# Masked softmax: the batches whose stores go out as a half and two quarters end with batch 5 instead of batch 7

## The chip, the cores and the metric

One core of a Trainium2 chip. The metric is the device time of one execution in microseconds (us), the median of several runs. The granted clock is 1.0 in all runs, and all are in the fast state, but for two of the four runs with stores of 64 partitions, which are said where they come.

A packet is one record of a DMA engine in the trace. A transfer has landed when the last of its semaphore records is in.

## The reference, cut to what matters

```python
batch, heads, seq_q, seq_k = 16, 8, 256, 256
x       = randn(batch, heads, seq_q, seq_k)            # float32
lengths = randint(seq_k // 2, seq_k, size=batch)
for b in range(batch):
    m = x[b, :, :, :lengths[b]]
    m = exp(m - max(m, axis=-1))
    result[b, :, :, :lengths[b]] = m / sum(m, axis=-1)  # zero beyond the length
```

One batch is 2 MB: 128 partitions of 16 rows of 256 values. It is loaded, masked, exponentiated, divided by its row sums and stored.

## The kernel before: the parts that matter

All loads and stores pass through eight slots in on-chip memory. Loads 0 to 3 are issued by the sync engine in full width. Loads 4 to 15 are issued by GpSimd, in a width rounded up from the batch's length, so their rows are short. Stores are issued by the sync engine, which waits for the division and, at the start of a batch, for the store of two batches before.

```python
def parts(b):
    if b == 0:                 cuts = [0, nt]
    elif b < 8:                cuts = [0, half, half + quarter, nt]   # nt = 16 rows
    elif b != batch - 3:       cuts = [0, half, nt]
    else:                      cuts = [0, nt]
    return [slice(i, j) for i, j in zip(cuts, cuts[1:])]
# ... (cut)
for b in range(batch):                                   # sync engine
    s_b = s_st[b % 2]
    for s in parts(b):
        nc.sync.wait_ge(s_out, 2 * b + (s.stop - 1) // half + 1)      # L117: divided
        if b >= 2 and s.start == 0:
            nc.sync.wait_ge(s_b, 64 * (b // 2 + 1))                   # L119: store b-2 landed
        nc.sync.dma_start(out=out_f[b, :, s, :], in_=xt[:, b % slots, s, :]   # L120
            ).then_inc(s_b, 16 * ((s.stop - s.start) // quarter))
# ... (cut) VectorE: the mask (L195) waits for the load; the division (L222) for the exponentials
for b in range(batch):
    at = 0 if b == batch - 2 else 2 if b == batch - 3 else 1 if b == 0 or b >= ahead else 0
    for h in range(3):
        if h == at and b + 1 < batch:
            mask(b + 1, slice(0, nt))
        if h < 2:
            divide(b, h)
```

The two quarters of a batch wait for the same count of `s_out`: neither can go before the other's rows are divided, and they differ from one half only in how the transfer is cut. Note `at`: batch 15 is masked before batch 14 is divided.

The softmax here doesn't subtract the row's maximum and nothing guards it: scores larger than these inputs give would overflow.

## Time and profile before

| | before |
|---|---|
| time, median of 3 runs | 156.04 us (155.91 to 156.53) |
| profiled span | 154.3 us |
| busy share of the 16 DMA engines, stores' queue and loads' queue | 66.0% and 32.2% |
| VectorE, ScalarE busy | 75%, 68% |

These two lines of the page before give GB/s in each of the 40 slices of the span, and the packets:

```profile
GB/s 117 427 450 420 437 365 409 400 408 452 407 406 390 415 404 417 412 413 415 405 419 413 414 412 405 416 416 420 417 416 423 418 431 435 418 444 418 423 431 130
DMA packets 10132, 62.08 MB, mean 402 GB/s; under 512 B 866, under 2 KB 962, under 8 KB 6290
```

No slice between the first and the last falls under 365. "Under 8 KB" holds the 4096 B packets of the quarters and the packets of the short-row loads. The prediction tells these apart by their records in the trace.

### The profile page before, as it was taken

Reading aid. Unit: us, or ns where it says so; the run is one execution under the profiler, and the core shown is the slowest. Engines: PE = TensorE matmul, PEld = TensorE weight load, DVE = VectorE, ACT = ScalarE, POOL = GpSimd, SP = SyncE. Lnnn points to the kernel's source line nnn. Section 1 sums busy time; section 2 is a strip of 40 time slices with the busy share of each in tenths; the row PEclk is TensorE's granted clock in tenths of the full one; section 3 lists DMA queues with packets and bytes.
Section 4 is the critical chain, followed back from the end, with each engine's and each line's share of the span. In section 5 each row is a group of like instructions: output and inputs, shape, how many; then the busy total and the mean of one; then the engine's idle time right before and its main releaser. Section 6 shows DMA issues by size and latency. Waiting matters only on the chain.

```text
span 154.3 us, 1325 instructions
## 1 busy us (share of the span) xinstructions
PE 0.2 (0%) x1; PEld 0.1 (0%) x1; DVE 115.4 (75%) x84; ACT 105.2 (68%) x514; POOL 19.0 (12%) x25
## 2 busy tenths in 40 slices
PE   0000000000000000000000000000000000000000
PEld 0000000000000000000000000000000000000000
DVE  1339999952999696988969696969698692599500
ACT  3097799992592969779595959596877907988000
POOL 4910031000320200202011020202010000000000
DMA  4999999999999999999999999999999999999993
GB/s 117 427 450 420 437 365 409 400 408 452 407 406 390 415 404 417 412 413 415 405 419 413 414 412 405 416 416 420 417 416 423 418 431 435 418 444 418 423 431 130
DMA packets 10132, 62.08 MB, mean 402 GB/s; under 512 B 866, under 2 KB 962, under 8 KB 6290
## 3 DMA queue, kind: packets, MB, share of 16 engines
q1 hardware_dynamic: 6048, 41.95, 66.0%
q0 software_dynamic: 4080, 20.12, 32.2%
q14 instruction: 2, 0.02, 0.0%
q10 hardware_dynamic: 2, 0.00, 0.0%
HBM read 28.51 MB, written 33.55 MB: 402 GB/s over the span
## 4 chain that ended last, share of the span: by engine, by line
DMA 54%; DVE 25%; issue 7%; ACT 5%; ACTq 2%; SPq 1%; POOLq 1%; DVEq 0%
DMA xt<-in_x_dram 33%; DMA out_dram<-xt 21%; DVE xt L222 14%; DVE xt L195 9%; ACT xt L251 5%; ACTq L251 1%; DVE inv_sum L219 1%; SPq L109 1%; POOLq L99 0%; SPq L120 0%; SPq L111 0%; DVEq L212 0%; POOLq L130 0%; POOLq L135 0%; ACTq L246 0%
## 5 line engine op out<-in xcount | busy, mean ns | idle before, releaser
L251 ACT ACTIVATE xt<-xt x256 | 102.3, 401 | 35.2 <-DVE xt L195 35.2
L222 DVE TENSOR_TENSOR xt<-xt,inv_sum 128x2048 f32<-128x2048 f32 x32 | 73.4, 2292 | 1.1
L195 DVE SCALAR_TENSOR_TENSOR xt<-down,len_s,xt 128x2048 f32<-128x2048 f32 (+1 forms) x17 | 37.8, 2221 | 14.1 <-DMA xt<-in_x_dram 14.0
L251 ACT ACTIVATION_READ_ACCUMULATOR xt<-xt x256 | 47.9, 187 | 0.0
L130 POOL DMA_DIRECT2D xt<-in_x_dram x12 | 12.8, 1064 | 94.6 <-issue 48.7
L219 DVE RECIPROCAL inv_sum<-row_sum 128x8 f32<-128x8 f32 x32 | 6.3, 198 | 12.1 <-ACT xt L251 12.1
L149 POOL MEMSET xt<- 128x1536 f32 x4 | 5.3, 1386 | 1.1 <-DVE len_s L186 1.1
L243 ACT ACT_TABLE_LOAD x1 | 1.3, 1283 | 1.6 <-SPq L81 1.6
L178 DVE TENSOR_SCALAR down<-iota_i 128x256 f32<-128x256 int32 x1 | 0.3, 297 | 1.6 <-POOL iota_i L141 1.6
L183 DVE CAST len_b<-word 1x16 bf16<-1x16 int32 x1 | 0.2, 164 | 0.4 <-DMA word<-in_lengths_dram 0.4
L186 DVE TENSOR_SCALAR len_s<-len_f 128x16 f32<-128x16 f32 x1 | 0.2, 174 | 0.4 <-PE len_f L165 0.4
L141 POOL IOTA iota_i<- 128x256 int32 x1 | 0.3, 332 | 0.6 <-SPq L81 0.6
L146 POOL MEMSET seed<- 1x1 f32 x2 | 0.3, 162 | 0.0
L243 ACT ACTIVATE warm<-const-float32-0.0 128x1 f32<-128x1 f32 x1 | 0.2, 203 | 0.0
L144 POOL MEMSET ones<- 1x128 bf16 x1 | 0.2, 194 | 0.0
L165 PE MATMUL len_f<-len_b,ones 1*128 1x16 bf16 x1 | 0.2, 168 | 2.6 <-DVE len_b L183 2.6
L274 POOL MEMSET const-float32-0.0<- 128x1 f32 x1 | 0.1, 98 | 0.3 <-issue 0.3
L165 PEld LDWEIGHTS len_f<-len_b,ones 1*128 1x128 bf16 x1 | 0.1, 97 | 2.6 <-POOL ones L144 2.6
L274 POOL MEMSET const-float32-1.0<- 128x1 f32 x1 | 0.1, 98 | 0.0
L274 POOL MEMSET const-bfloat16-1.0<- 128x1 bf16 x1 | 0.1, 98 | 0.0
L274 POOL MEMSET const-uint8-127<- 128x1 uint8 x1 | 0.1, 98 | 0.0
L274 POOL BASE_LOAD x1 | 0.0, 17 | 0.1
## 6 DMA issues: line engine op xcount, KB each, us to landing
out_dram<-xt SPq DMA_DIRECT2D x21, 1024.0 KB
out_dram<-xt SPq DMA_DIRECT2D x14, 512.0 KB
xt<-in_x_dram SPq DMA_DIRECT2D x3, 2048.0 KB, 16.0
xt<-in_x_dram POOLq DMA_DIRECT2D x3, 1728.0 KB, 16.5
out_dram<-xt SPq DMA_DIRECT2D x2, 2048.0 KB
xt<-in_x_dram POOLq DMA_DIRECT2D x2, 2048.0 KB, 18.4
xt<-in_x_dram POOLq DMA_DIRECT2D x2, 1600.0 KB, 16.7
xt<-in_x_dram POOLq DMA_DIRECT2D x2, 1280.0 KB, 14.5
```

The source lines that it names most:

```text
L109: nc.sync.dma_start(out=xt[:, 0, s], in_=x_f[0, :, s]).then_inc(s_ld[h], 16)
L130: nc.gpsimd.dma_start(out=xt[:, slot, :, :w], in_=x_n[:, n, :, :w]).then_inc(s_sw[par], 16)
L141: nc.gpsimd.iota(iota_i, pattern=[[1, seq_k]], base=0, channel_multiplier=0).then_inc(s_iota, 1)
L146: nc.gpsimd.memset(seed[:, par : par + 1], 0.0).then_inc(s_st[par], 64)
L149: nc.gpsimd.memset(xt[:, b, :, low:], 0.0).then_inc(s_fill, 1)
L165: nc.tensor.matmul(len_f, lhsT=ones, rhs=len_b, start=True, stop=True).then_inc(s_lenf, 1)
L195: return nc.vector.scalar_tensor_tensor(out=t, in0=down[:, None, lo:hi].to_broadcast([P, s.stop - s.start, hi - lo]), scalar=len_s[:, b : ...
L219: step(nc.vector.reciprocal(out=inv_sum[:, b, s], in_=row_sum[:, b, s]))
L222: nc.vector.tensor_tensor(out=t, in0=t, in1=inv_sum[:, b, s, None].to_broadcast([P, half, seq_k]), op=ALU.mult,).then_inc(s_out, 1)
L243: nc.scalar.activation(out=warm, in_=nc.const_aps.tensor(0.0, (P, 1), F32), func=EXP)
L251: ins = nc.scalar.activation(out=e, in_=e, func=EXP, accum_out=sum_h[:, bass.ds(i, 1), j])
L274: nc = _bacc.Bacc("TRN2", target_bir_lowering=False, num_devices=1)
```

## The change

Intent: two transfers fewer, and larger packets, in batches 6 and 7. The whole diff:

```diff
-        elif b < 8:
+        elif b < 6:
             cuts = [0, half, half + quarter, nt]
```

## The prediction

> **What bounds the kernel now.** I read the page first, then the waits, the busy time by stretch, and the chain of waits at the end.
>
> From the page:
>
> ```profile
> span 154.3 us, 1325 instructions
> DMA  4999999999999999999999999999999999999993
> q1 hardware_dynamic: 6048, 41.95, 66.0%
> q0 software_dynamic: 4080, 20.12, 32.2%
> out_dram<-xt SPq DMA_DIRECT2D x21, 1024.0 KB
> out_dram<-xt SPq DMA_DIRECT2D x14, 512.0 KB
> ```
>
> The 16 DMA engines are full in 38 of 40 slices, and the two queues fill 98.2% of the span. So 62 MB of traffic is the bound, and only what leaves the DMA engines empty, or makes packets dearer, can cost time. q1 carries the first four loads and then all stores; q0 carries the other twelve loads. The 14 stores of 512 KB are the quarters of batches 1 to 7.
>
> The waits, of the engines and of the queue that issues stores:
>
> ```profile
> DVE xt L195 <- DMA xt<-in_x_dram: 14.0, 4, 4.8
> SPq L119 <- DMA out_dram<-xt: 91.7, 14, 9.6
> SPq L120 <- DVE xt L222: 12.6, 9, 3.3
> ```
>
> VectorE waits for a load only four times. The store issuer waits mostly for the store of two batches before (L119): stores stand in a backlog, and compute runs ahead of them.
>
> The chain of waits, its last stretch:
>
> ```profile
> 115.19 17.53 DMA xt<-in_x_dram
> 132.95 2.35 DVE xt L195
> ...
> 135.45 2.29 DVE xt L222
> ...
> 137.89 2.29 DVE xt L222
> ...
> 140.33 2.29 DVE xt L222
> ...
> 142.77 2.29 DVE xt L222
> ```
>
> Here that changes. The last load (batch 15) lands at 132.72 us, and the mask and four divisions of batches 14 and 15 follow without a gap up to 145.06, which is 12.34 us after the landing. The last store is issued at 145.09. By the trace's semaphore records it lands at 153.08, 8.0 us later, because batches 13 and 14 are still ahead of it in the queue. The first load, a 1 MB half on an empty queue, needed 1.13 to 6.20, or 5.07 us. So the last store has about 8.0 - 5.07 = 2.9 us of **slack**: the last load can be that much later before the end moves. This rests on the estimate that a lone 1 MB store takes as long as that lone 1 MB load.
>
> **How the queues share the engines.** The trace's packet records show a store packet of 8192 B for a half (mean 313 ns) and of 4096 B for a quarter (163 ns), and load packets of about 4.4 KB (171 to 177 ns) made of several short rows. In 50 to 100 us I count 2038 store packets and 2160 load packets; in 100 to 120 us, with halves alone, 647 and 690. The ratio is 1.06 and 1.07[...]. So the size of a store packet decides who gets the bandwidth. While a quarter is being stored, loads get about half; while a half is, about a third.
>
> [...]
>
> ```profile
> 84.00:89.37 5.37, 0.00 (x0) 0.00 (x0) 4.19 (x4) 5.37 (x29) 0.00 (x0) 1.00 1.03 415
> 93.46:98.90 5.44, 0.00 (x0) 0.00 (x0) 4.26 (x4) 4.77 (x24) 1.15 (x1) 1.00 1.03 410
> 98.90:102.85 3.95, 0.00 (x0) 0.00 (x0) 3.37 (x3) 2.74 (x14) 0.00 (x0) 1.00 1.01 413
> 102.85:106.84 3.99, 0.00 (x0) 0.00 (x0) 3.36 (x3) 3.75 (x20) 1.15 (x1) 1.00 1.02 419
> ```
>
> The first two stretches run from the landing of a batch's half to that of its second quarter (batches 6 and 7), the last two are the halves of batch 8. The last column is GB/s: 410 to 415 against 413 to 419, nearly the same total, but the same 1 MB of stores takes 5.4 us in quarters and 3.97 us as a half. [...]
>
> **The change, part by part.**
>
> Removed: for batches 6 and 7, four quarter stores become two halves, so two issues fewer on the sync engine (about 0.4 us each when not held up, by the trace). That engine waits 91.7 us for stores; this is worth nothing. Both quarters wait for the same division (the wait rounds up to the whole second half), so no store starts earlier or later because of the form itself.
>
> Packets: 512 packets of 4096 B become 256 of 8192 B, 16 fewer pairs per engine: 16 x (2 x 163 - 313) = 16 x 13 ns = **0.2 us** less DMA work over the whole kernel. This is the whole direct gain.
>
> Moved: stores of the second halves of batches 6 and 7 go at 3.97 instead of 5.4 us, so batch 7 lands about 2.9 us sooner (96.0 instead of 98.9). Loads pay. In 83.3 to 88.5 and 92.8 to 98 us, quarters against loads, each engine took 15.94 + 15.75 load packets in 10.4 us: 328 ns each. From 98.9 to 122.8, halves against loads, all engines took 829 in 23.87 us: 461 ns each. The quarters run beside about 32 x 1.07 = 34 load packets per engine. With halves these need 34 x (461 - 328) = **4.5 us** more. I take 4.6, since a count of pure turns (32 x (3.97/8 - 5.4/16) us) gives 5.1.
>
> Does the loss stay? Loads get it back only if the store queue runs empty. After the change batch 8 is issued at about 88 (batch 6 landed, division done at 85.55), batch 9 at 96 and so on; each store issue still finds about one batch queued. Only the masks are held up: loads 10 and 11 land some 2.3 and 3.5 us later, loads 12 to 15 4.6 us later. Load 10 landed 0.8 us before its mask, load 13 0.5 us and loads 14 and 15 right at it, so VectorE now waits for every load from 10 on. The divisions of batches 9 to 12 ended 3.8 us or more before their stores were issued; now the stores are due 2.9 us sooner and the masks come 2 to 4.5 us later, so batches 11 and 12 can be issued 1 to 4 us late. But one whole batch (8 us) is in flight at each issue, so the queue doesn't run dry there. By conservation, loads and the stores up to batch 12 are both done by about 138.1, as they are before (batch 12 lands at 138.28); what has changed is that the loads come last with them instead of 5 us earlier.
>
> At the end: last load at 132.72 + 4.6 = 137.3; last division at 137.3 + 12.34 = 149.7; last store lands at 149.7 + 5.07 = 154.8 instead of 153.08. That is 4.6 - 2.9 = **+1.7 us**. By then only batch 13 is queued: it ends at about 138.1 + 4.95 = 143.1 (it took 138.28 to 143.24), and the halves of 14 and 15 come at the pace of the divisions (2.44 us each), which is just that of the DMA. So the engines run out of work once, when batch 13 has drained and the first half of 14 is only being issued, around 143 to 145.
>
> Sum: 156.04 + 1.7 = 157.7 us. The 0.2 us of saved packets falls before the last load and could take a little off; a slow engine or a store slower than a load could add. I say **157.7 us**.
>
> **Rivals.** *Hidden anyway:* the end is set by total traffic; with 0.2 us less work it would be 155.8. For it speak 38 full slices and 2.9 us of slack; against it, that the loss of 4.6 us is larger than the slack. It needs the loads to lose less than 2.9 us. *Whole loss on the path:* if the slack is mostly an artefact [...] or the store queue runs dry in the 110s because masks come late, the end moves by 3.5 to 4.6 us: 159.5 to 160.6. Against it: the batch in flight at each issue. *Fewer, larger stores are faster:* [...] 1% of the rate over the 10.8 us of quarters would be 0.1 us. Even the mixed stage at 413 and the later one at 418 GB/s differ in load widths too. It cannot reach 2%.
>
> **Range and chances.** The loss of loads is 4.0 to 5.1 us, the slack 2 to 3.2 us, so the end moves by 0.8 to 3.1, and for what I have not seen (loads catching up in a gap of the store queue) I go lower: 156.4 to 159.1. The 2% mark is 159.16, which needs the second rival in part: 0.09. Faster by 2% needs 152.9 us, below the traffic bound: 0.01. Within 2%: 0.90.
>
> **What would show it.** Right: 35 stores instead of 37, 23 of 1024 KB and 10 of 512 KB; the same load landings up to about 83 us; the wait of the mask (L195) for loads up from 14.0, with more than four times; the last load landing near 137.3; the last store landing some 5 us after its issue, with a DMA slice below 9 near 143. The load share of the traffic from 83 to 98 us falls from about half to a third. Wrong: if load 15 lands before about 135.6, the end should not move; if it lands at 137 and the end still doesn't move, a lone store is faster than 5 us; if the time rises by 4 us, the slack was none.

The sum is 156.04 + 1.7 = 157.7 us, with 1.7 = 4.6 - 2.9 from the trace's counts and times and from the estimate that a lone store takes as long as a lone load. The "pure turns" of the 5.1 us are an estimate too: exactly one load packet to one store packet, where 1.06 and 1.07 were counted. By the packet records, loads moved 51% of the bytes beside quarters (83.3 to 88.5 us) and 37% beside halves (98.9 to 122.8 us). The lines that follow a cut there without a word before them are busy time by stretch, with GB/s last.

## The result and the profile after

Ratios are the mean time of one kernel's fast runs over that of the other's of the same rounds, so not quite the ratio of the medians.

| | before | after |
|---|---|---|
| time, median | 156.18 us (155.91 to 156.53, 4 runs) | 158.0 us (157.91 to 158.38, 4 runs) |
| ratio | | 1.012 (95%: 1.009 to 1.015) |
| profiled span | 154.3 us | 156.8 us |
| last load lands | 132.72 us | 139.10 us |
| last store lands (its issue) | 153.08 (145.09) | 155.52 (151.47) |
| store of batch 7 lands | 98.90 | 95.91 |
| store of batch 12 lands | 138.28 | 138.57 |

Landings are from the semaphore records of the trace. The change costs 1.8 us of the median: 1.2%, inside 2%. The profiled run is the slowest of the four (158.38).

From the page after:

```profile
span 156.8 us, 1323 instructions
DMA  3999999999999999999999999999999999991995
GB/s 111 424 443 422 443 406 414 395 404 443 405 399 401 391 413 423 406 419 407 413 429 407 420 417 412 413 413 420 420 412 425 414 416 449 424 443 63 426 410 226
DMA packets 9844, 62.08 MB, mean 396 GB/s; under 512 B 834, under 2 KB 930, under 8 KB 5746
out_dram<-xt SPq DMA_DIRECT2D x23, 1024.0 KB
out_dram<-xt SPq DMA_DIRECT2D x10, 512.0 KB
```

The bytes are the same. The transfers are fewer by two, as they should be. The full row of nines now has a hole: slice 37 (from 141.1 to 145.0 us) at "1" and 63 GB/s.

Busy time by stretch, after (last two columns: DMA share and GB/s). The first two stretches are the second halves of batches 6 and 7, now one transfer each; the last two are the hole and what follows it:

```profile
84.07:88.06 3.99, 0.00 (x0) 0.00 (x0) 2.80 (x3) 3.99 (x21) 0.00 (x0) 1.00 1.02 420
91.83:95.91 4.08, 0.00 (x0) 0.00 (x0) 4.04 (x3) 1.51 (x7) 1.16 (x1) 1.00 1.02 415
143.02:144.99 1.97, 0.00 (x0) 0.00 (x0) 1.94 (x3) 1.97 (x11) 0.00 (x0) 1.00 0.00 0
145.00:155.20 10.20, 0.00 (x0) 0.00 (x0) 6.38 (x5) 3.43 (x18) 0.00 (x0) 1.00 0.98 408
```

The halves take 4.0 and 4.1 us, where the quarters took 5.4, at nearly the same total rate (415 to 420 GB/s, and 410 to 415 before). For 1.97 us nothing moves at all; then 4 MB of stores go out.

The waits after, of VectorE and of the sync engine:

```profile
DVE xt L195 <- DMA xt<-in_x_dram: 19.5, 8, 5.3
```

```profile
SPq L119 <- DMA out_dram<-xt: 75.6, 13, 8.6
SPq L120 <- DVE xt L222: 34.9, 17, 5.5
```

Before, the mask waited four times for a load (14.0 us in all); now eight times. The store issuer still waits most for earlier stores (75.6 us, 91.7 before), but 34.9 us for divisions instead of 12.6: stores now wait in part for loads.

The chain of waits after, its last stretch:

```profile
121.09 18.01 DMA xt<-in_x_dram
...
139.33 2.35 DVE xt L195
...
149.15 2.29 DVE xt L222
```

It is the same chain as before, 6.4 us later: load 15, the mask, four divisions. It takes 12.34 us from the landing to the last division, to the hundredth what it took before (151.44 - 139.10).

Where did the time go? By the packet records from 83 to 98 us, loads moved 2.95 MB before and 2.32 MB after, stores 3.22 and 3.96 MB. The sum is the same within 2%; the loads' part falls from 48% to 37%. At the end, the loads that were pushed back finish together with the store of batch 12, and only one 2 MB store is left to cover the chain that follows the last load. It isn't long enough: the store queue is empty from 143.02 us, and the first half of batch 14 is issued at 144.15.

### The profile page after: what moved, and what is told of

It reads as the page before. It is cut to its first block, busy times and chain, and to the rows that moved or that the text cites. A ratio compares the mean times of both kernels' runs of the same rounds, so it can differ in the third digit from the quotient of the medians.

```text
span 156.8 us, 1323 instructions
## 1 busy us (share of the span) xinstructions
PE 0.2 (0%) x1; PEld 0.1 (0%) x1; DVE 115.9 (74%) x84; ACT 105.2 (67%) x514; POOL 19.0 (12%) x25
## 4 chain that ended last, share of the span: by engine, by line
DMA 79%; DVE 8%; issue 5%; POOLq 3%; SPq 1%; POOL 0%; DVEq 0%
DMA xt<-in_x_dram 79%; DVE xt L222 6%; DVE xt L195 2%; POOLq L99 1%; POOLq L135 1%; POOLq L130 1%; SPq L109 1%; POOL xt L130 0%; DVE inv_sum L219 0%; SPq L111 0%; POOLq L157 0%; POOLq L153 0%; POOLq L159 0%; POOLq L137 0%; DVEq L212 0%
```

## The experiments

**Theory A**: about one load packet moves per store packet, of 4096 B as of 8192 B (1.06 from 50 to 100 us, where 1315 of 2038 store packets have 4096 B, and 1.07 from 100 to 120 us, where all have 8192 B), so the size of a store packet sets the loads' share; the end moves only by what the loads lose beyond a slack at the end. Rivals: B, a cost in proportion to the batches in halves; C, the number or size of transfers matters, not their packets; others below. All results were correct. Ratios are against the kernel before on the same chip.

### Half of the change

```diff
-        elif b < 8:
+        elif b < 7:
```

> Half of the change: quarters end with batch 6, so only batch 7 goes in halves. Theory A (a store packet's size sets the loads' share; the end moves only by the loads' loss beyond the slack at the end): the loads lose half of what they lost in the change (some 2.7 us), the slack is 8.0 - 4.05 = 3.9 us, so the last load lands near 135.5 and the time is that of the kernel before, ratio 0.998 to 1.003 (156.1 us). Theory B (cost in proportion to the number of batches in halves, no slack): half the loss of time, 157.1 us, ratio 1.006.

Measured: 156.02 us (6 runs), ratio 0.9999 (0.998 to 1.001). The last load of the profile lands at 135.16, the last store at 153.06. From its page, and its busy time where the changed kernel stood still:

```profile
DMA  4999999999999999999999999999999999999993
```

```profile
142.00:146.00 4.00, 0.00 (x0) 0.00 (x0) 3.93 (x5) 2.49 (x14) 0.00 (x0) 1.00 1.00 424
```

The end did not move, and there is no hole: B falls, and the slack exists. That the loads lost half, 2.4 us by this profile, is not shown: a profile of the kernel before with only its tail edited, which comes below, has its last load at 135.02 without any loss.

### The change carried on: three, then four batches in halves

```diff
-        elif b < 8:
+        elif b < 5:      # the second kernel: b < 4
```

> The change carried on: quarters end with batch 4, so batches 5, 6 and 7 go in halves. Theory A: the loads lose another 2.7 us, and with the slack already used up all of it shows: 158.0 + 2.7 = 160.7 us, ratio 1.028. Theory B (in proportion): 158.0 + 0.9 = 158.9 us, ratio 1.018.

Measured: 159.42 us (4 runs), ratio 1.021 (1.019 to 1.023). Between the two numbers, and both missed. The last load lands at 140.51 and the last store at 156.90. The end followed the load; what fell short was the load's delay. I had counted another 2.7 us from the changed kernel, whose one profile until then was of its slowest run (the second one, in the next section, has load 15 at 138.01, and 2.5 us to 140.51). Counted from the one profile of the kernel before, 7.8 us for three batches is 2.6 us each.

> Quarters end with batch 3, so batches 4 to 7 go in halves. The last load came 2.6 us later per batch in halves (7.8 us for three). Theory A: the fourth batch adds 2.0 to 2.6 us, one for one on the end: 161.4 to 162.0 us, ratio 1.034 to 1.038. Rival G (the store queue runs dry while masks wait for loads, and the loads then catch up, so that the loss levels off; this would explain that the third batch cost only 1.4 us): 160.4 us or less, ratio at most 1.028.

Measured: 159.28 us (4 runs), ratio 1.019 (1.017 to 1.022), last load 139.98, last store 156.41. A's number is missed; rival G holds. The waits of the sync engine in this kernel:

```profile
SPq L120 <- DVE xt L222: 64.7, 19, 7.4
SPq L119 <- DMA out_dram<-xt: 49.1, 9, 8.3
```

The issuer now waits more for divisions than for stores. By the packet records the store queue has four gaps between 100 and 131 us (104.07 to 104.39, 112.53 to 112.87, 121.20 to 121.44, 129.54 to 130.70). Of the milder kernels only the one with three batches in halves has any there, of 0.17 us (129.51 to 129.68). In a gap the loads have the engines to themselves (the slices of the page that hold the gaps stay at "9", with 395 to 439 GB/s). This fits a loss that limits itself: late loads delay masks, masks delay stores, and stores that are late give the loads their bandwidth back. No run takes the gaps away to test it.

### The changed kernel again

No edit.

> The changed kernel unchanged, beside the next three on the same chip: 158.0 us, ratio 1.012. Its last load lands between 138.0 and 139.5 (139.1 in the first profile, 138.3 in the one with the cut tail).

Measured: 157.77 us (157.3 to 158.52, 6 runs), ratio 1.012. Last load 138.01, last store 154.44. This profile was of the fastest of its six runs, the first one of the slowest of its four. Its pause:

```profile
143.06:143.90 0.84, 0.00 (x0) 0.00 (x0) 0.81 (x2) 0.84 (x5) 0.00 (x0) 1.00 0.00 0
```

0.84 us instead of 1.97, in the same program: the landing of loads differs from run to run. In the first profile load 8 already landed 0.9 us late (71.86 against 70.96), before the change can act.

The kernel before has such a second profile too: that of the edited tail below, whose edit acts only after load 15 has landed. Its load 15:

```profile
117.45 17.57 DMA xt<-in_x_dram
135.02 0.03 issue
```

135.02 here and 132.72 in the first profile, for the same program up to this point. The changed kernel has five profiles that are alike up to this point (two of its own, three with edited tails): 138.01, 138.09, 138.22, 138.31 and 139.10. So the loads lost between 3.0 and 6.4 us, and two profiles don't say it more closely; that all five lie after both profiles of the kernel before is clear.

### Where the knee is

All profiles whose tail is not edited, by the landing of the last load:

| kernel | last load | last store | last store minus last load |
|---|---|---|---|
| more quarters (below) | 127.49 | 153.39 | 25.90 |
| before | 132.72 | 153.08 | 20.36 |
| large 4096 B packets (below) | 133.62 | 153.04 | 19.42 |
| one batch in halves | 135.16 | 153.06 | 17.90 |
| quarters moved (below) | 135.33 | 153.07 | 17.74 |
| changed, again | 138.01 | 154.44 | 16.43 |
| changed | 139.10 | 155.52 | 16.42 |
| four batches in halves | 139.98 | 156.41 | 16.43 |
| three batches in halves | 140.51 | 156.90 | 16.39 |
| stores of 64 partitions (below) | 141.15 | 157.58 | 16.43 |

From 132.72 to 135.33 the last store stands still at 153.06 within 0.02 us (with more quarters it is 0.3 later, by the work of their packets, see below). From 138.01 on it follows the last load at 16.4 us. The two lines meet at 153.06 - 16.42 = 136.64: this is the knee. So the slack of the kernel before was 136.64 - 132.72 = 3.9 us in the first profile, and 1.6 us in the run with load 15 at 135.02. The knee is firm; the landing differs from run to run.

### Is it the packet, or the transfer?

The second halves of batches 6 and 7 again as two 512 KB transfers each, but with 8192 B packets:

```diff
+                if b in (6, 7) and s.start == half:
+                    for p in (slice(0, P // 2), slice(P // 2, P)):
+                        nc.sync.dma_start(out=out_f[b, p, s, :],
+                            in_=xt[p, b % slots, s, :]).then_inc(s_b, 16)
+                    continue
```

> The changed kernel, but the second halves of batches 6 and 7 are again stored as two 512 KB transfers each, cut by partitions (64 and 64), so that the packets stay at 8192 B. Number, size and order of the transfers are those of the kernel before, the packets those of the changed one. Theory A (packet size): as the changed kernel, 158.0 us, ratio 1.012. Theory C (the number or size of transfers, or how many increments of a semaphore are in flight, is what matters): as before, 156.1 us, ratio 1.00.

Measured: 160.45 and 161.52 us in two runs, some 1.03 of the kernel before; the other two, 163.63 and 164.26, are slow (the median 162.58 and ratio 1.041 hold all four). Neither theory says this. Its busy time, in the stretch of these transfers and after:

```profile
84.00:96.00 12.00, 0.00 (x0) 0.00 (x0) 5.64 (x4) 5.43 (x28) 0.76 (x1) 1.00 1.02 373
96.00:120.00 24.00, 0.00 (x0) 0.00 (x0) 19.73 (x15) 18.94 (x94) 2.71 (x3) 1.00 1.01 398
```

373 GB/s, where the changed kernel has 415 to 420 while its halves go out. By the packet records the 8192 B store packets took 376 ns (84 to 89 us) and 354 ns (93 to 99.4), where the changed kernel has 313 and 315: transfers of 64 partitions are themselves slower here, so this run doesn't separate A from C. Why they are slower is not shown.

The opposite way does. Changed kernel, with batch 6 as two 1 MB transfers whose packets are all 4096 B:

```diff
+        out_g = out_f.rearrange("b p (a g j) k -> b p a g (j k)", a=2, g=2)
+        xt_g = xt.rearrange("p s (a g j) k -> p s a g (j k)", a=2, g=2)
+                if b == 6:                       # after both divisions
+                    if s.start == 0: continue
+                    for g in range(2):
+                        nc.sync.dma_start(out=out_g[b, :, :, g],
+                            in_=xt_g[:, b % slots, :, g]).then_inc(s_b, 32)
+                    continue
```

> The changed kernel, with batch 6 stored as two 1 MB transfers, each of every other group of four rows, so that all its packets are of 4096 B (512 packets, as many as the four removed quarters had); batch 7 stays in halves. Two transfers per batch, as in the changed kernel, packets in sum as before. Theory A: as before, 156.1 us, ratio 0.998 to 1.004, last load near 133. Theory C: as the changed kernel, 158.0 us, ratio 1.012.

Measured: 156.03 us (4 runs), ratio 1.000 (0.998 to 1.002), last load 133.62. Its trace has the same packets on the store queue as the kernel before (1792 of 4096 B, 2944 of 8192 B), in as many transfers as the changed kernel. The time is that of the kernel before, and load 15 lands as early as in its two profiles. C falls.

### The same quarters, later

```diff
-        elif b < 6:
+        elif b < 6 or b in (8, 9):
```

> Quarters in batches 1 to 5 and 8 and 9 instead of 1 to 7: the same number of quarters, two batches later. Theory A: the loads lose 5 us from batch 6 on and win it back beside the quarters of 8 and 9, so loads 10 to 12 land late but 14 and 15 on time (15 near 133), and the time is that of the kernel before, ratio 0.998 to 1.005. Rival D (it is the late loads 10 and 11 and the masks waiting for them that cost the time): near the changed kernel, ratio 1.01.

Measured: 156.20 us (4 runs), ratio 1.002 (0.999 to 1.004). Load 10 lands at 91.36, as late as in the changed kernel (91.56), but load 15 at 135.33, under the knee. D falls: late loads in the middle cost nothing. I had expected load 15 near 133. The time doesn't tell, because of the slack, and neither does the landing, with 132.72 and 135.02 in the kernel before.

### More quarters

```diff
-        elif b < 8:
+        elif b < 12:
```

> The change the other way: quarters up to batch 11. Theory A: the loads land earlier still (load 15 about 8 us sooner, near 125, if nothing else holds it up), but the end of the kernel before is set by the traffic, so nothing is won; the four batches' small packets add 4 x 8 x 2 x 13 ns or less: some 0.4 us. 156.1 to 156.6 us, ratio 1.000 to 1.003. Rival B (in proportion, no slack): 156.1 - 3.6 = 152.5 us, ratio 0.977.

Measured: 156.81 us (4 runs), ratio 1.005 (1.003 to 1.008). Load 15 lands 5.2 us earlier, at 127.49, and nothing is won: with the loads early, the traffic is the bound (DMA is at "9" in all 38 slices between the first and the last). The cost of the small packets was larger than I had said: per engine, the packets of 4096 and 8192 B on the sync engine's queue add up to 76.89 us instead of 76.25, 0.64 more. My 0.4 is 4 x 8 pairs of 13 ns; the formula as I wrote it, with a further factor of 2, gives 0.8.

### The tail: which of its parts holds the end?

Three edits of the last two batches. The first divides and stores the second half of batch 15 in two quarters:

```diff
+        if b == batch - 1: cuts = [0, half, half + quarter, nt]     # parts
+            n = quarter if b == batch - 1 and h == 1 else half      # divide
+            for i in range(s.start, s.stop, n): # ... (cut: multiply rows i to i + n, s_out + 1;
+            # the store of the last quarter waits for one count more)
```

> The changed kernel with the second half of the last batch divided and stored in two quarters. Theory A says that its end is the chain last load, mask, divisions, lone store: the last store then has 512 KB and lands some 1.2 us sooner after its issue, so about 156.8 us, ratio 1.004. If its end were set by traffic (rival E), nothing moves: 158.0, ratio 1.012.

> The kernel before with the same edit of the last batch as e8_tail_after. Theory A: its end is set by the queue of stores, not by the last division, so nothing moves: 156.1 us, ratio 0.998 to 1.003. If the chain of divisions set the end before too (rival F), it gains 1.2 us, ratio 0.992.

Measured on the changed kernel: 157.67 us (6 runs), ratio 1.011, so nothing against 1.012. On the kernel before: 156.41 us, ratio 1.002, so the edit costs 0.3 there. My 1.2 us, an estimate (half of the prediction's 2.44 us for 1 MB is 1.2), failed. In the trace the reason is plain: after the pause, four stores start one behind the other, and they land at 147.32, 149.77, 152.23, then 153.53 and 154.81 for the quarters. The quarters are issued at 149.61 and 150.75, behind a half that is issued at 148.24 and lands at 152.23, so cutting the last one makes no difference: it stands in line. So rival E's number came true: after the pause, traffic and divisions run at the same pace (2.45 us from landing to landing, 2.44 from division to division).

The second edit fills the pause by dividing the first half of batch 14 before waiting for load 15; the third is both.

```diff
-            at = 0 if b == batch - 2 else 2 if b == batch - 3 else 1 if ...
+            at = 1 if b == batch - 2 else 2 if b == batch - 3 else 1 if ...
```

> The changed kernel, but VectorE divides the first half of batch 14 before it waits for load 15 and masks batch 15. Its store is then issued near 140 instead of 144, so the DMA engines don't run dry at 143. Theory H (after the pause, four 1 MB stores stand in line, and the pause is what sets the end): 1.5 to 2 us off, 156.2 to 156.5 us, ratio 1.002. Theory I (the chain last load, mask, exponentials, last division, lone store is as long, whatever else is in line): hardly anything, 157.8 to 158.0 us, ratio 1.011.

> Both edits, the order of e10_order_after and the quarters at the end of e8_tail_after. With the pause filled and the last store cut to 512 KB, both limits move: theory I expects 1 to 1.2 us less than the changed kernel, 156.8 to 157.0 us, ratio 1.005. Theory H expects no more than the order alone gives.

Measured: order alone 157.87 us (6 runs), ratio 1.012; both 157.34 us (6 runs), ratio 1.008 (1.006 to 1.010), beside 157.77 and 1.012 of the changed kernel itself. The page of the order alone:

```profile
DMA  4999999999999999999999999999999999999675
```

The hole is no longer one hole: its last slices but one are a little empty instead. The pause was a symptom. With it filled, the engines wait between the last divisions (147.79 to 148.45 and 151.12 to 151.64 in the packet records), since load 15, its mask, its exponentials and its two divisions still take their time (2.35 us for a mask and 2.29 for a division in the chain of the first profile after). Theory H falls, I holds for this run; of I's 1 to 1.2 us for both edits only 0.4 came, with intervals that just overlap; by the issue times the first half of batch 15 is then the next to stand in line. No version here beats the kernel before.

## Why the prediction was right

The time was 158.0 us where 157.7 was predicted, within the range, and it went the way named: late loads, past the slack. That it is so near is in part luck, as two terms were off and nearly cancelled. By its steps:

- **About one load packet per store packet, of either size.** Right as a count: from 83 to 98 us there are 684 load packets to 635 store packets before (1.08) and 533 to 483 after (1.10), records of 4 B left out. Batch 7 landed at 95.91 (predicted 96.0), at nearly the same total rate (415 GB/s in the stretch of its second half, 410 before); the kernel with large transfers of small packets (156.03 us, last load 133.62) shows that packets, not transfers, do it. In which order an engine takes the packets of its queues is not shown: the packet records of the trace name the queue and not the engine.
- **Direct gain, 0.2 us.** Not found. The packets of 4096 and 8192 B on the sync engine's queue add up to 76.25 us per engine before and 76.39 after. The term was an average of packet times over other stretches, too small to hold.
- **What the loads lose, 4.6 us.** Neither confirmed nor refuted as a size: 3.0 to 6.4 us by two profiles of the kernel before and five of the changed one. The last load was put at 137.3; it landed at 138.01 to 139.10, 0.7 to 1.8 us later. Part of this is the run.
- **The slack, 2.9 us.** Mis-sized: 3.9 in the same profile. The step that failed is the estimate that a lone 1 MB store takes as long as the first 1 MB load (5.07 us). The first half of batch 14 in the changed kernel, issued at 144.15 into an empty queue, landed at 148.12, after 3.97 us; the last store took 151.47 to 155.52, 4.05 us. So the knee was put at 132.72 + 2.9 = 135.6 and lies at 136.6. The 1.0 us here and the 0.7 to 1.8 us above nearly cancel: 1.4 to 2.5 us past the knee, around the 1.7 predicted.
- **Two readings.** The last store before was said to stand behind batches 13 and 14. At its issue (145.09) batch 13 had landed (143.24); ahead of it were batch 14 and the first half of 15. The 8.0 us and the slack stand. And the 38 full slices run from 365 to 452 GB/s, with a median of 416 (I had read 410 to 430, in a sentence now cut; 21 of them lie there).
- **The loss stays, as the store queue doesn't run dry.** Right for this change, where the store queue has no gap before the pause; with four batches in halves it has four.
- **Compute up to the last division, 12.34 us after the last load.** Exact.
- **The hole near 143 us.** Seen, 143.02 to 144.99 and 143.06 to 143.90. But it is not what costs: filled by another order, the time stays.
- **Rivals.** "Hidden anyway" holds for half of the change, exactly (1.000). "The slack is an artefact" is false: it is larger than I took it to be. "Fewer, larger stores are faster" did not show: 415 to 420 GB/s beside 410 to 415 in these stretches, and a longer time.

What stays open: why the landing of the loads differs by 1.1 to 2.3 us between runs of one program, and how large the loss is apart from it; and why the packets of the 64-partition stores are slow.

## What to carry to other kernels

In this kernel, with two DMA queues backed up, the packet size of one was a throttle on the other at a nearly constant total rate (from 83 to 98 us, the loads' part of the bytes fell from 48% to 37%, with the sum the same within 2%): where you find the same, give the smaller packets to the stream that may wait. Find the knee before you size such a change: measure how far the last load's chain ends ahead of the drained queue, with the time of a lone store of the right kind, because here a loss up to that slack (3.9 us in the first profile) was free and beyond it counted in full (the last store 16.4 us after the last load). Profile each kernel more than once before you read a difference of landings. The hole in the busy row (1.97 and 0.84 us) appeared here once the slack had run out, and was not by itself what there was to gain: filled, it left the time at 157.87 us beside 157.77.
